# GpSimd's splits and factors in two layers go to VectorE, and its share of the scan's decay masks to ScalarE

## The chip, the core and the metric

The kernel runs on one core of a Trainium2 chip. The engines of the core that matter here are TensorE (PE in the profile, with its weight loads as PEld), VectorE (DVE), ScalarE (ACT) and GpSimd (POOL); SyncE (SP) issues the loads. Each engine works through its own instructions in order, and they wait for one another by semaphores. The metric is the device time of one execution in microseconds (us). Before the change it was 2820.69 us, the median of three runs (2819.77 to 2827.25).

## The reference, cut to what matters

The whole program is two blocks one after the other on 256 tokens of width 1024: a first block of two layers (feed-forward, token mixer, feed-forward), and a second block of two layers, one "even" and one "odd", each a mixer followed by a feed-forward network with a convolution. The change touches the two mixers of the second block.

The even mixer has gated linear attention. Per head it computes, in chunks,

```
cum = jnp.cumsum(lac, axis=1)
rel = jnp.where(tri, cum[:, :, None] - cum[:, None, :], -jnp.inf)
att = jnp.einsum('bthk,bshk,btshk->bhts', qc, kc, jnp.exp(rel))
o = jnp.einsum('bhts,bshv->bthv', att, vc) + jnp.einsum('bthk,bhkv->bthv', qc * jnp.exp(cum), s)
```

in both directions, for the context tokens first and then for the latent tokens, beside an mLSTM scan. The odd mixer has a state-space scan in four groups of eight heads:

```
cum = jnp.cumsum(dtc * A, axis=1)
seg = jnp.where(tri, cum[:, :, None] - cum[:, None, :], -jnp.inf)
cb = jnp.einsum('btgn,bsgn->btsg', cc, bc)
w = jnp.exp(seg) * cb[..., None] * dtc[:, None]
y = jnp.einsum('btsgh,bsghp->btghp', w, xc) + ...
```

Both mixers begin and end with dense products of the tokens with weight matrices in float32.

## The kernel before, in words

**Weights.** Every dense product is made in three passes, from a high and a low part of each operand. A weight tile of 1 MB lands in `raw`; `wsplit` (L411) makes from each half of it the high part `wh` on ScalarE and then the low part `wl` = `raw` - `wh`, a subtraction of 128 x 1024 elements, on VectorE or on GpSimd. Which one is decided by a counter: `lo_pool` = 5 sends every fifth low part to GpSimd, 3 every third, 2 every second, 0 none. It is 0 in the first block, 5 in the even mixer (L1875), 2 in the first convolution network (L1888), 3 in the odd mixer (L1890) and 1.15 in the last network (L1894). There are three buffers each of `raw`, `wh` and `wl`.

**Linear attention** (`gla`, L1218). For each of two pairs of heads and each of two directions it makes the exponentials `Z` (tile `gz`) of seven levels, and then the factors of each level by `factors(i)`: one product of `gz` with the keys on 128 partitions and two with the queries on 64 partitions each, into the tile `gqd`, which has room for four levels. Levels 2 and 5 go to GpSimd, the others to VectorE. `pair_scores` multiplies a level's factors on TensorE and copies the results under a mask to `gs` on VectorE (L830), and asks for the factors of level i + 4 when level i is done. Over context and latents these are 8 passes.

**The scan** (`odd_group`, L1726). For each of 4 groups, 2 token tiles and 2 halves of the heads, the decay exponents of four heads are summed on TensorE in the PSUM tile `aux` from four masked products `oR` (128 x 512): for each direction one from the high part of the decays (`dAh`) on GpSimd, and one from the low part (`dAl`) on VectorE. ScalarE takes the exponential into `oE`, VectorE multiplies it by `oD` (the time steps) and by `cbm`, and TensorE multiplies it with `ox`. `oy`, `oz`, `ow`, `st` and `oss` are the tiles of the rest of the scan; `oss` gets its power -0.5 on GpSimd (`rstd`, L520). Beside it runs `odd_in` of the next group, which evacuates a product `mm` as a convolution into `tof`: one step on ScalarE, two on VectorE, a tanh on ScalarE back into `mm`, and one more step on VectorE.

**Order.** The mixers' generators are woven into one another (`weave`), and a scheduler then lays down each engine's instructions in one fixed order when the program is built. Small powers (`hss`, `mss`, `rsd`, `mv`) stay on GpSimd everywhere.

The helpers are `mul`, `sub` and `tt` (all L173), `stt` (L185), `ts` (L189, L191), `act` (L194) and `mm` (L167), so that most rows of the profile bear a helper's line, and the tile's name tells the place.

Of the kernel before, what the change touches and what calls it, by code (L numbers as in the profile page):

```python
# [14 lines left out]
AF = mybir.ActivationFunctionType  # L15
# [104 lines left out]
class _K:  # L120
# [1096 lines left out]
    def gla(self, o, s, gp, Y):  # L1217

        nc = self.nc
        lah, lal, qT, kT, v, sil = (o[k] for k in ("lah", "lal", "qT", "kT", "v", "sil"))  # L1220
        dirs = (("cf", "sf", 0), ("cb", "sb", 1))

        Q = gp.tile([128, 2, 4, 2, 64], F32, tag="gqd", name="gqd", bufs=1)
        nc.gpsimd.memset(Q, 0.0)
        for j in range(2):
            ZF = gp.tile([128, 2, 2, 128], F32, tag="gzf", name="gzf", bufs=1)

            S = gp.tile([128, 2, 2, 128], F32, tag="gs", name="gs", bufs=1)
            X = gp.tile([128, 2, 2, 128], F32, tag="gx", name="gx", bufs=1)
            nc.gpsimd.memset(S, 0.0)  # L1230
            kv = kT[:, j].rearrange("p (t s) -> p t s", t=2)
            qv = qT[:, j].rearrange("p (t s) -> p t s", t=2)
            for qc, kc, d in dirs:
                Z = gp.tile([128, 2, 8, 128], F32, tag="gz", name="gz", bufs=1)
                cs = slice(d * 256 + j * 128, d * 256 + j * 128 + 128)
                for t in range(2):
                    late = t == (1 - d)
                    mm2 = lambda p, c, tt, a, b: (self.mm(p, lah[:, tt, cs], c, a, False),
                                                  self.mm(p, lal[:, tt, cs], c, False, b))
                    p = self.ps([128, 512], "acc")  # L1240
                    mm2(p, self.lev[:, d * 896:d * 896 + 512], t, True, True)
                    self.act(Z[:, t, 0:4].rearrange("p a b -> p (a b)"), p, AF.Exp)
                    p = self.ps([128, 512], "acc")
                    mm2(p[:, :384], self.lev[:, d * 896 + 512:(d + 1) * 896], t, True, True)
                    mm2(p[:, 384:], self.wr(qc if late else kc), t, True, True)
                    self.act(Z[:, t, 4:8].rearrange("p a b -> p (a b)"), p, AF.Exp)
                    p = self.ps([128, 128], "acc")
                    other = (not late) if s else late
                    mm2(p, self.wr(kc if s else qc), t, True, not other)
                    if other:  # L1250
                        mm2(p, self.wr("ones"), 1 - t, False, True)
                    self.act(ZF[:, d, t], p, AF.Exp)
                    yield
                l_, r_ = (kv, qv) if d == 0 else (qv, kv)
                def factors(i):
                    L = LEVELS[i]
                    eng = nc.gpsimd if i % 3 == 2 else None
                    z, k_, q_ = (self.halves(a, L) for a in (Z[:, :, i, :], kv, qv))
                    self.mul(z[d], z[d], k_[d], eng)
                    for e in range(2):  # L1260
                        pr = slice(e * 64, e * 64 + 64)
                        q = Q[pr, :, i % 4, e].rearrange("p t (b c) -> p t b c", c=L // 2)
                        self.mul(q, z[1 - d][pr], q_[1 - d][pr], eng)
                for i in range(4):
                    factors(i)
                self.mul(Z[:, 0, 7], Z[:, 0, 7], l_[:, 0])
                self.mul(Z[:, 1, 7], Z[:, 1, 7], r_[:, 1])
                self.mul(ZF[:, d], ZF[:, d], kv if s else qv)
                yield
                self.pair_scores(Z, Q, S.rearrange("p e t c -> p (e t) c"), d, kv, qv, factors)  # L1270
                yield
                for e in range(2):
                    pr = slice(e * 64, e * 64 + 64)
                    p = self.ps([128, 128], "acc")
                    self.mm(p, Z[pr, d, 7], Z[pr, 1 - d, 7])
                    self.act(X[:, e, d], p)
                yield
                if s:
                    ke = self.tmp([128, 2, 128], "g")
                    p = self.ps([128, 2, 128], "acc")  # L1280
                    for t in range(2):
                        nc.tensor.transpose(p[:, t], ZF[:, d, t], self.ident)
                    nc.vector.tensor_copy(ke, p)
                    p = self.ps([128, 256], "acc")
                    for t in range(2):
                        self.mm(p, ke[:, t], v[:, t, j * 256:(j + 1) * 256], t == 0, t == 1)
                    nc.vector.tensor_copy(self.gla_state[:, d, j], p)
                    yield
            for e in range(2):
                pr = slice(e * 64, e * 64 + 64)  # L1290
                h = 2 * j + e
                hv = slice(h * 128, h * 128 + 128)
                po = self.ps([128, 2, 128], "acc")
                for t in range(2):
                    self.mm(po[:, t], S[:, e, t], v[:, t, hv], True, False)
                    self.mm(po[:, t], X[:, e, 1 - t], v[:, 1 - t, hv], False, bool(s))
                    if not s:
                        for d in range(2):
                            self.mm(po[:, t], ZF[pr, d, t], self.gla_state[pr, d, j, e * 128:(e + 1) * 128], False, d == 1)
                self.head_norm(po, sil[:, :, hv])  # L1300
                yield
        for _ in self.rows_to_T(sil, [self.col("gla_norm_g_2", k) for k in range(4)], Y, "acc"):
            yield
# [420 lines left out]
    def odd_group(self, o, g, K, gp, Y, big):  # L1724

        nc = self.nc  # L1726
        I32 = mybir.dt.int32
        x, z, BT, Br, CT = (o[k] for k in ("x", "z", "B", "Br", "C"))
# [14 lines left out]
        for d in range(2):  # L1743
            t = d
# [10 lines left out]
        for t in range(2):  # L1755
# [11 lines left out]
            for hq in range(2):  # L1767
                h0 = g * 8 + hq * 4
                pe = self.ps([128, 512], "aux")
                for d, (cc, sc) in enumerate((("cf", "sf"), ("cb", "sb"))):  # L1770
                    for i, a in enumerate(K["dAr"]):
                        R = gp.tile([128, 4, 128], F32R, tag="oR", name="oR", bufs=4)
                        self.mul(R, self.c(cc)[:, None, :].to_broadcast([128, 4, 128]),
                                 self.bc8(a[:, t, d * 32 + h0:d * 32 + h0 + 4], 128), None if i else nc.gpsimd)
                        self.mm(pe, self.wr(sc), R.rearrange("p a b -> p (a b)"), d + i == 0, d + i == 2)
                E = gp.tile([128, 4, 128], F32, tag="oE", name="oE", bufs=1)
                self.act(E.rearrange("p a b -> p (a b)"), pe, AF.Exp)
                dm = gp.tile([128, 4, 128], F32, tag="oD", name="oD", bufs=1)
                self.act(dm, self.bc8(dt[:, t, h0:h0 + 4], 128))
                m = self.c("sf").bitcast(I32)  # L1780
                nc.vector.copy_predicated(out=dm, mask=m[:, None, :].to_broadcast([128, 4, 128]),
                                          data=self.bc8(dt[:, t, 32 + h0:36 + h0], 128))
                self.mul(E, E, dm)
                self.mul(E, E, cbm[:, None, :].to_broadcast([128, 4, 128]))
                for a in range(4):
                    c0 = (hq * 4 + a) * 64
                    self.mm(py[:, c0:c0 + 64], E[:, a], x[:, t, c0:c0 + 64])
                yield
# [75 lines left out]
    def second_block(self):  # L1864

        xc = self.dram.tile([128, 2, D], F32, name="xc")
        with self.tc.tile_pool(name="second", bufs=1) as self.sp:
            with self.tc.tile_pool(name="evenT", bufs=1) as self.hp:
                self.hl = self.pair(self.hp, KT, T, "hl")
                self.operand(5, self.hl)  # L1870
                self.sub_block(5, self.hl, False, lambda: self.load_context(self.sp, self.hp))
                self.run(self.filler)
                self.gctx.__exit__(None, None, None)
                self.r = self.cur
                self.lo_pool = 5  # L1875
                ss, css = self.even(xc)
            self.dump("s000", self.r)
            self.dump("s100", xc)
# [7 lines left out]
    def layers(self, xc, ss):  # L1886
        r = self.r
        self.lo_pool = 2  # L1888
        ss = self.conv_ffn(0, ss, xc)
        self.lo_pool = 3  # L1890
        self.dump("s001", r)
        ss = self.odd()
        self.dump("s010", r)
# [49 lines left out]
```

## Time and profile before

| | before |
|---|---|
| median of three runs | 2820.69 us |
| the profiled execution | 2826.35 us, span 2824.6 us |
| PE busy | 2588.0 us (92%) |
| DVE busy | 2185.3 us (77%) |
| ACT busy | 1238.0 us (44%) |
| POOL busy | 435.0 us (15%) |
| even mixer, 1458 to 1815 us | PE 320.6 of 357 us, DVE 260.4, POOL 68.6 |
| first convolution network, 1852 to 2205 us | PE 353.0 of 353 us |
| odd mixer, 2205 to 2545 us | PE 305.6 of 340 us, DVE 270.2, POOL 92.3 |

Busy times are sums over one engine and say nothing of who waits for whom. The waits of an engine in a stretch do, and the rows of the timeline in which one instruction lasts longer than its like.

### The profile page before, as it was taken

To read this page: it belongs to the slowest core of one execution; us is meant where nothing else is said; L and a number is where in the kernel's file an instruction comes from. 1 tells how busy PE (TensorE), PEld (TensorE's weight loads), DVE (VectorE), ACT (ScalarE), POOL (GpSimd) and SP (SyncE) were. 2 spreads that over 40 slices of the span, in tenths; PEclk is the share of its full clock that TensorE was granted. 3 is DMA by queue.
4 is the path that set the end of the run, shared out by engine and by line. 5 is a ranking of instruction groups with operands and counts; after the bars stand their busy time and mean duration, and the time that the engine had idled before them with its cause. 6 is when DMAs were issued, how large, how long until landed. Compare 5 with 4: busy or idle time off the path is not lost. (4 is left out here: it accounts for less than half of the span.)

```text
span 2824.6 us, 42561 instructions
## 1 busy us (share of the span) xinstructions
PE 2588.0 (92%) x16403; PEld 2287.1 (81%) x16403; DVE 2185.3 (77%) x4073; ACT 1238.0 (44%) x1983; POOL 435.0 (15%) x310
## 2 busy tenths in 40 slices
PE   7997999899899999989998998999999999988887
PEld 6886998799799899879987787778888777757776
DVE  6778997987878999897566857778487478886775
ACT  3444444544444454444445463444233544334443
POOL 0000010000000001000011212212122223234564
PEclk9999999999999999999999999999999999999999
DMA  9898777888888886787572141432223322224443
GB/s 317 284 327 280 243 231 265 261 299 294 279 277 274 269 263 200 257 298 234 187 227 81 34 154 42 151 110 90 90 90 97 102 75 75 83 64 145 141 155 108
DMA packets 374360, 526.31 MB, mean 186 GB/s; under 512 B 24721, under 2 KB 279565, under 8 KB 373005
## 3 DMA queue, kind: packets, MB, share of 16 engines
q1 hardware_dynamic: 372389, 522.83, 56.4%
q8 instruction: 129, 2.11, 0.3%
q10 hardware_dynamic: 1768, 0.76, 0.1%
q14 instruction: 74, 0.61, 0.1%
HBM read 512.46 MB, written 11.08 MB: 185 GB/s over the span
## 5 line engine op out<-in xcount | busy, mean ns | idle before, releaser
L194 ACT ACTIVATE wh<-raw 128x1024 fp32r<-128x1024 f32 x665 | 699.6, 1056 | 916.3 <-PE mm L167 392.5
L173 DVE TENSOR_TENSOR wl<-raw,wh 128x1024 fp32r<-128x1024 f32 (+1 forms) x544 | 666.2, 1229 | 275.8 <-ACT wh L194 272.3
L167 PE MATMUL mm<-hTh,wh 128*128 128x256 f32 (+2 forms) x2200 | 677.0, 308 | 29.0 <-DVE gl L173 8.0
L167 PE MATMUL mm<-hTh,wl 128*128 128x256 f32 (+2 forms) x2200 | 667.1, 303 | 11.4 <-DVE wl L173 11.4
L167 PE MATMUL mm<-hTl,wh 128*128 128x256 f32 (+2 forms) x2200 | 666.9, 303 | 1.3 <-DVE hTl L173 1.3
L167 PEld LDWEIGHTS mm<-hTh,wh 128*128 128x128 f32 (+1 forms) x2200 | 423.0, 192 | 53.6 <-DVE gl L173 10.5
L167 PEld LDWEIGHTS mm<-hTh,wl 128*128 128x128 f32 (+1 forms) x2200 | 422.2, 192 | 30.0 <-DVE wl L173 14.3
L167 PEld LDWEIGHTS mm<-hTl,wh 128*128 128x128 f32 (+1 forms) x2200 | 422.6, 192 | 19.0 <-issue 3.2
L173 POOL TENSOR_TENSOR wl<-raw,wh 128x1024 fp32r<-128x1024 f32 x121 | 293.0, 2426 | 620.3 <-ACT wh L194 594.3
L185 DVE SCALAR_TENSOR_TENSOR graw<-graw,cb 128x1024 f32<-128x1024 f32 x224 | 272.7, 1220 | 36.9 <-DMA graw<-in_c_adaT_dram 31.6
L185 DVE SCALAR_TENSOR_TENSOR fo<-mm,colv,fo 128x189 f32<-128x189 f32 (+3 forms) x396 | 170.1, 430 | 37.6 <-ACT fo L194 35.3
L185 DVE SCALAR_TENSOR_TENSOR fo<-aux,colv,fo 128x189 f32<-128x189 f32 (+3 forms) x396 | 170.2, 430 | 9.7 <-ACT fo L194 6.2
L167 PE MATMUL acc<-wl,gh 128*128 128x512 f32 x352 | 139.2, 395 | 1.6 <-DVE wl L173 1.6
L167 PE MATMUL acc<-wh,gh 128*128 128x512 f32 x352 | 139.5, 396 | 0.6 <-DVE r L173 0.5
L167 PE MATMUL acc<-wh,gl 128*128 128x512 f32 x352 | 138.6, 395 | 0.0
L167 PE MATMUL acc<-wh,cg 128*128 128x512 f32 x396 | 136.2, 403 | 1.9 <-ACT wh L194 1.9
L167 PE MATMUL aux<-hTh,wh 128*128 128x512 f32 (+1 forms) x352 | 120.2, 341 | 14.7 <-DVE cg L173 14.7
L167 PE MATMUL mm<-hlh,wh 128*128 128x256 f32 (+1 forms) x456 | 129.6, 285 | 4.0 <-ACT hlh L194 1.9
L167 PE MATMUL mm<-hlh,wl 128*128 128x256 f32 (+1 forms) x456 | 129.4, 284 | 0.0
L167 PE MATMUL mm<-hll,wh 128*128 128x256 f32 (+1 forms) x456 | 129.1, 283 | 0.0
L167 PE MATMUL aux<-hTh,wl 128*128 128x512 f32 (+1 forms) x352 | 118.8, 338 | 0.0
L167 PE MATMUL mm<-wh,hTh 128*128 128x256 f32 x384 | 112.3, 293 | 7.1 <-ACT hTh L194 3.5
(557 smaller groups left out, 5303.5 us busy)
## 6 DMA issues: line engine op xcount, KB each, us to landing
raw<-in_ffn_w_in_dram SPq DMA_DIRECT2D x88, 1024.0 KB
graw<-in_c_adaT_dram SPq DMA_DIRECT2D x128, 512.0 KB
raw<-in_mix_w_in_dram SPq DMA_DIRECT2D x52, 1024.0 KB
graw<-in_c_modT_dram SPq DMA_DIRECT2D x96, 512.0 KB
raw<-in_ffn_w_up_dram SPq DMA_DIRECT2D x44, 1024.0 KB
raw<-in_ffn_w_out_dram SPq DMA_DIRECT2D x40, 1024.0 KB
raw<-in_even_w_in_dram SPq DMA_DIRECT2D x28, 1024.0 KB
raw<-in_ffn_w_down_dram SPq DMA_DIRECT2D x20, 1024.0 KB
```

The costliest lines, as they stand in the source:

```text
L167: self.nc.tensor.matmul(out, lhsT, rhs, start=start, stop=stop)
L173: (eng or self.nc.vector).tensor_tensor(out=out, in0=a, in1=b, op=op)
L185: self.nc.vector.scalar_tensor_tensor(out, a, s, b, op0=op0, op1=op1, **kw)
L194: self.nc.scalar.activation(out, a, f, **kw)
```

## The change: three edits

The factors of levels 2 and 5 go from GpSimd to VectorE with the others. In the scan, the masked product of the high part becomes four ScalarE instructions of 128 x 128, one for each head, each of which scales the mask by a column. `lo_pool` is 0 in both mixers, so that all their low parts are made on VectorE; the two convolution networks keep theirs.

```diff
                 def factors(i):
                     L = LEVELS[i]
-                    eng = nc.gpsimd if i % 3 == 2 else None
                     z, k_, q_ = (self.halves(a, L) for a in (Z[:, :, i, :], kv, qv))
-                    self.mul(z[d], z[d], k_[d], eng)
+                    self.mul(z[d], z[d], k_[d])
                     for e in range(2):
                         pr = slice(e * 64, e * 64 + 64)
                         q = Q[pr, :, i % 4, e].rearrange("p t (b c) -> p t b c", c=L // 2)
-                        self.mul(q, z[1 - d][pr], q_[1 - d][pr], eng)
+                        self.mul(q, z[1 - d][pr], q_[1 - d][pr])
...
                         R = gp.tile([128, 4, 128], F32R, tag="oR", name="oR", bufs=4)
-                        self.mul(R, self.c(cc)[:, None, :].to_broadcast([128, 4, 128]),
-                                 self.bc8(a[:, t, d * 32 + h0:d * 32 + h0 + 4], 128), None if i else nc.gpsimd)
+                        if i:
+                            self.mul(R, self.c(cc)[:, None, :].to_broadcast([128, 4, 128]),
+                                     self.bc8(a[:, t, d * 32 + h0:d * 32 + h0 + 4], 128))
+                        else:
+                            for h in range(4):
+                                c0 = d * 32 + h0 + h
+                                self.act(R[:, h], self.c(cc), AF.Copy, scale=a[:, t, c0:c0 + 1])
...
                 self.r = self.cur
-                self.lo_pool = 5
                 ss, css = self.even(xc)
...
         ss = self.conv_ffn(0, ss, xc)
-        self.lo_pool = 3
+        self.lo_pool = 0
         self.dump("s001", r)
         ss = self.odd()
```

The scheduler lays the instructions in a new order from the start of the even mixer on. Three places show it.

On GpSimd, from the start of the even mixer into the first passes of linear attention, before:

```order
L523 TENSOR_TENSOR mv<-mv,mhalf 128x1 x2
L173 TENSOR_TENSOR wl<-raw,wh 128x1024
L523 TENSOR_TENSOR rsd<-rsd,mhalf 128x2
L173 TENSOR_TENSOR wl<-raw,wh 128x1024 x2
L173 TENSOR_TENSOR gz<-gz,gk 128x2x16x4
L173 TENSOR_TENSOR gqd<-gz,gq 64x2x64 x2
L173 TENSOR_TENSOR gz<-gz,gk 128x2x2x32
L173 TENSOR_TENSOR gqd<-gz,gq 64x2x64 x2
L1325 MEMSET mll 128x8x2
```

and now:

```order
L523 TENSOR_TENSOR mv<-mv,mhalf 128x1 x2
L523 TENSOR_TENSOR rsd<-rsd,mhalf 128x2
L1324 MEMSET mll 128x8x2
L523 TENSOR_TENSOR mss<-mss,mhalf 128x2
L1230 MEMSET gs 128x512
L523 TENSOR_TENSOR hss<-hss,mhalf 128x2 x2
```

Nothing but memsets and small powers stays on GpSimd there.

On VectorE, the factors of the first pass of linear attention (`gz` and `gqd`, with the width of a level's blocks in the shape), before:

```order
L173 TENSOR_TENSOR gqd<-gz,gq 64x2x64 x2
L173 TENSOR_TENSOR gz<-gz,gk 128x2x32x2
L173 TENSOR_TENSOR gqd<-gz,gq 64x2x64 x2
L173 TENSOR_TENSOR gz<-gz,gk 128x2x8x8
L173 TENSOR_TENSOR gqd<-gz,gq 64x2x64 x2
L173 TENSOR_TENSOR gz<-gz,gq 128x128
L173 TENSOR_TENSOR gzf<-gzf,gk 128x256
L173 TENSOR_TENSOR gz<-gz,gk 128x2x4x16
L173 TENSOR_TENSOR gz<-gz,gk 128x2x64
L173 TENSOR_TENSOR wl<-raw,wh 128x1024
L830 COPY_PREDICATED gs<-mask,acc 128x256
```

and now:

```order
L173 TENSOR_TENSOR gz<-gz,gk 128x2x32x2
L173 TENSOR_TENSOR gqd<-gz,gq 64x2x64 x2
L173 TENSOR_TENSOR gz<-gz,gk 128x2x16x4
L173 TENSOR_TENSOR gqd<-gz,gq 64x2x64 x2
L173 TENSOR_TENSOR gz<-gz,gk 128x2x8x8
L173 TENSOR_TENSOR gqd<-gz,gq 64x2x64 x2
L173 TENSOR_TENSOR gz<-gz,gq 128x128
L173 TENSOR_TENSOR gzf<-gzf,gk 128x256
L830 COPY_PREDICATED gs<-mask,acc 128x256
L173 TENSOR_TENSOR gz<-gz,gk 128x2x4x16
L173 TENSOR_TENSOR gqd<-gz,gq 64x2x64 x2
L173 TENSOR_TENSOR gz<-gz,gk 128x2x2x32
```

Level 2 (blocks of 4, 128x2x16x4) now stands between levels 1 and 3, and level 5 (128x2x2x32) among the masked copies.

On ScalarE, the third step of the scan's first group, with the convolution `tof` of the next group, before:

```order
L194 ACTIVATE wh<-raw 128x1024
L194 ACTIVATE tof<-mm,colv 128x512
L194 ACTIVATE oy,oss<-oz 128x512
L194 ACTIVATE oE<-aux 128x512
L194 ACTIVATE mm<-tof 128x512
L194 ACTIVATE oD<-dt_21818 128x512
L194 ACTIVATE ox<-gv 128x4x128
```

and now:

```order
L194 ACTIVATE wh<-raw 128x1024
L194 ACTIVATE tof<-mm,colv 128x512
L194 ACTIVATE oy,oss<-oz 128x512
L194 ACTIVATE oR<-levr,dAh 128x128 x4
L194 ACTIVATE mm<-tof 128x512
L194 ACTIVATE oR<-levr,dAh 128x128 x4
L194 ACTIVATE oE<-aux 128x512
L194 ACTIVATE oR<-levr,dAh 128x128
L194 ACTIVATE ox<-gv 128x4x128
```

The masked products stand before and behind the tanh (`mm<-tof`), and some before the evacuation of `gv` into `ox`.

## Rows read from the trace of the kernel before

**Rows 1.** The page's first line: the profiled span.
```profile
span 2824.6 us, 42561 instructions
```

**Rows 2.** Stretches: length, busy us of PE, PEld, DVE, ACT, POOL; PEclk, DMA, GB/s.
```profile
1458.00:1815.00 357.00, 320.60 (x2167) 283.29 (x2166) 260.38 (x595) 170.21 (x359) 68.59 (x84) 0.96 0.30 95
1852.00:2205.00 353.00, 353.00 (x1525) 286.33 (x1524) 248.35 (x541) 125.56 (x161) 77.07 (x32) 1.00 0.29 93
2205.00:2545.00 340.00, 305.60 (x1563) 238.44 (x1562) 270.20 (x426) 145.00 (x229) 92.30 (x59) 0.96 0.26 80
```

**Rows 3.** Waits of PE, 1458 to 1815 us: total us, times, longest.
```profile
PE acc L167 <- DVE gqd L173: 5.7, 6, 2.1
...
PE acc L167 <- DVE gs L830: 5.5, 5, 1.9
...
PE aux L1387 <- DVE silu L173: 3.2, 2, 2.8
```

**Rows 4.** Waits of PE, 2205 to 2545 us.
```profile
PE aux L942 <- DVE oz L189: 5.9, 4, 3.1
PE acc L167 <- ACT mm L194: 4.3, 4, 2.1
...
PE gv L1711 <- DVE tof L185: 4.2, 5, 1.6
PE acc L167 <- DVE ow L173: 3.5, 4, 1.6
```

**Rows 5.** Groups on DVE, 2205 to 2545 us: count, busy us, mean ns.
```profile
L173 DVE TENSOR_TENSOR oR<-levr,dAl 128x512 fp32r<-128x512 f32 x32 | 27.6, 874 | 13.9 <-PE aux L167 13.8
...
L173 DVE TENSOR_TENSOR oE<-oE,oD 128x512 f32<-128x512 f32 x16 | 16.6, 1039 | 0.7 <-ACT oE L194 0.7
...
L173 DVE TENSOR_TENSOR oy<-oy,ow 128x512 f32<-128x512 f32 x16 | 10.9, 684 | 0.1
...
L173 DVE TENSOR_TENSOR oy<-ox,coef 128x512 f32<-128x512 f32 x8 | 10.1, 1267 | 0.0
...
L173 DVE TENSOR_TENSOR hTl<-ogy,hTh 128x1024 fp32r<-128x1024 f32 x3 | 3.7, 1218 | 0.3 <-ACT hTh L194 0.3
```

**Rows 6.** Timeline at 2523 us: start, length, instruction, wait before.
```profile
2523.59 2.34 POOL L173 TENSOR_TENSOR wl<-raw,wh 128x1024 fp32r<-128x1024 f32 x1
2523.66 2.56 DVE L189 TENSOR_SCALAR oz<-oz,oss 128x512 f32<-128x512 f32 x1 [0.44 <-POOL oss L523]
...
2526.36 0.45 PE L942 MATMUL aux<-small,oz 128*128 128x128 f32 x1 [3.06 <-DVE oz L189]
```

**Rows 7.** Timeline at 1692 us.
```profile
1691.98 2.36 POOL L173 TENSOR_TENSOR wl<-raw,wh 128x1024 fp32r<-128x1024 f32 x1 [17.28 <-ACT wh L194]
1692.13 2.75 DVE L1368 TENSOR_TENSOR_SCAN g<-small,nmst,g 4x256 f32<-4x256 f32 x1
```

**Rows 8.** Stretches behind PE's longer waits, columns as in rows 2.
```profile
1694.50:1701.00 6.50, 5.55 (x27) 4.75 (x28) 5.84 (x16) 0.57 (x2) 2.86 (x4) 0.50 0.00 0
...
sum 45.00, PE 41.00 PEld 35.98 DVE 32.35 ACT 9.47 POOL 10.66; mean PE 5.12 PEld 4.50 DVE 4.04 ACT 1.18 POOL 1.33
```

**Rows 9.** Groups on POOL, whole span.
```profile
L173 POOL TENSOR_TENSOR wl<-raw,wh 128x1024 fp32r<-128x1024 f32 x121 | 293.0, 2426 | 620.3 <-ACT wh L194 594.3 <-issue 16.4 <-DVE fo L185 9.0
L173 POOL TENSOR_TENSOR oR<-levr,dAh 128x512 fp32r<-128x512 f32 x32 | 41.3, 1305 | 98.8 <-PE aux L167 91.2 <-ACT dAh L194 7.6
```

**Rows 10.** Groups on DVE, 1480 to 1815 us.
```profile
L173 DVE TENSOR_TENSOR gqd<-gz,gq 64x128 f32<-64x128 f32 x80 | 26.0, 325 | 1.0
L173 DVE TENSOR_TENSOR gz<-gz,gk 128x128 f32<-128x128 f32 x48 | 14.8, 314 | 1.9 <-ACT gz L194 1.1
```

**Rows 11.** Groups on ACT of 128 x 128 elements, whole span.
```profile
L194 ACT ACTIVATE krw<-krw,mecols 128x128 f32<-128x128 f32 x16 | 5.9, 397 | 5.5 <-DVE krw L1405 3.0 <-PE aux L167 2.4
...
L194 ACT ACTIVATE dAh<-dA 128x128 fp32r<-128x128 f32 x1 | 0.3, 289 | 0.0
```

**Rows 12.** Waits of ACT, 2205 to 2545 us.
```profile
ACT wh L194 <- PE mm L167: 57.5, 28, 6.5
```

## The prediction

> **What bounds the kernel now.** I read the stretches first. In the first convolution network TensorE is busy for all of its 353 us at the full clock; nothing that another engine does there can shorten it [rows 2]. The two mixers are different: in the even one TensorE stands for 357 - 320.6 = 36.4 us, in the odd one for 340 - 305.6 = 34.4 us, with a granted clock of 0.96 over both [rows 2]. These two stretches are all that the change touches, so 70.8 us of standing, and what the clock loses behind it, is what can be won. VectorE is the engine next to it: 260.4 of 357 and 270.2 of 340 us, 73% and 79%; ScalarE has 48% and 43%, GpSimd 19% and 27% [rows 2].
>
> Next come TensorE's waits in the two stretches. Nearly all are for VectorE or for a ScalarE step that itself stands in a chain with VectorE: in the odd mixer for `oz`, the tanh back into `mm`, `tof` and `ow`, together 5.9 + 4.3 + 4.2 + 3.5 = 17.9 us [rows 4]; in the even one for `gqd`, `gs` and `silu`, 5.7 + 5.5 + 3.2 = 14.4 us [rows 3]. So VectorE's latency sets the pace of the mixers, and not its mean load.
>
> Then the groups of VectorE, to see why it is late. Products of the same form, 128 x 512 from two tiles, take 684 ns in one group (`oy<-oy,ow`), but 874 ns (`oR`), 1039 ns (`oE<-oE,oD`) and 1267 ns (`oy<-ox,coef`) in others [rows 5]. The timeline shows what makes the difference: at 2523.66 us a VectorE step on `oz` lasts 2.56 us, to 2526.22; a low part on GpSimd ran from 2523.59 to 2525.93, and the step ended 0.29 us behind it. TensorE stood 3.06 us for that `oz` [rows 6]. At 1692.13 a prefix sum over four partitions lasts 2.75 us and ends 0.54 us behind a low part on GpSimd [rows 7]; it leads to the wait of 2.8 us for `silu` [rows 3]. VectorE is held up by GpSimd until that one's instruction is over. And the stand has an echo: the stretch behind this wait, and seven like it, run at 0.50 of the clock, the lower of its two levels (1.2 GHz), 45 us in all [rows 8].
>
> **The odd mixer, part by part.** Removed from GpSimd: 32 products `oR` of 1305 ns and, by the order of the new program, 20 of the 31 low parts of 2426 ns that leave it [rows 9]. GpSimd's own time there was no bound. What VectorE gets back: 32 x (874 - 684) = 6.1 us, 16 x (1039 - 684) = 5.7, 8 x (1267 - 684) = 4.7, so 16.5 us from three groups alone [rows 5]. The upper end is GpSimd's busy time there, 92.3 us [rows 2]. I take 30, nearer to the lower end, since other groups have smaller excesses of the same kind. What VectorE gets: 20 low parts at 1218 ns, the price of the same subtraction in `hTl<-ogy,hTh` [rows 5], 24.4 us. So its load stays or falls a little, and pieces of 1.2 us that stand in the order take the place of hold-ups of up to 2 us that no order foresees. What ScalarE gets: 32 x 4 = 128 small products. The old trace has none. The nearest rows are `krw`, 128 x 128 scaled by a column, 397 ns, and `dAh`, a plain copy into the same type, 289 ns [rows 11]: 37 to 51 us. I take 397 ns, since it has the scaling too: 50.8 us, and ScalarE goes from 145 to 196 of 340 us. That is covered as long as ScalarE has the new pieces done while VectorE works on `tof` between the evacuation and the tanh, where the new order puts four of them.
>
> On TensorE: of the 17.9 us above and the smaller waits of the same chains I take 12 as hold-ups that go, since the one in rows 6 alone is worth 2, and 6 us as coming back, as VectorE's known work grows by 24.4 us and ScalarE's queue gets longer. Net -6. Below: nothing goes and 6 come, +6. Above: all of 17.9 go, -17.9.
>
> **The even mixer, part by part.** 11 low parts go to VectorE, 11 x 1.218 = 13.4 us. The factors: 8 passes of two levels each, one product of 314 ns and two of 325 ns [rows 10], 8 x 2 x 0.964 = 15.4 us. That is 28.8 us on VectorE, 260.4 to 289.2 less the hold-ups. Of these the step of rows 7 shows some 2 us; GpSimd's busy time of 68.6 us is the upper end [rows 2]; an estimate from the odd mixer's share, 30 of 92.3, gives 22. So VectorE gets some 7 us more here. On TensorE I take 7 us as going (the waits for `silu` and parts of those for `gqd`), and 5 as coming, since levels 2 and 5 were made beside VectorE and now stand in its line, with the masked copies `gs` and the products that TensorE waits for queued behind them. Net -2; bounds +12 (nothing goes, 12 of the 28.8 us show) and -14.4 (all of the three rows).
>
> **The clock.** The eight stretches of 45 us at 0.50 cost up to half of that, 22.5 us [rows 8], as TensorE was busy for 41 of them. All eight stand in the mixers, behind waits. With the longest waits gone I take a third of it, -8; bounds 0 and -22.5.
>
> **The sum.** -6 - 2 - 8 = -16 us. The profiled execution took 2826.35 us with a span of 2824.6 [rows 1], so it becomes 2810.35. It lies 5.66 us above the median of the runs, 2820.69, so that the median becomes 2804.7, which I round to 2805.
>
> **A rule that speaks against it.** The low parts on GpSimd take 2426 ns on the mean of 121, twice the 1218 ns on VectorE [rows 5, 9], and it is VectorE that was late in both timelines [rows 6, 7]. The Trainium skill, in "SBUF — State Buffer", section "Who interferes with whom", says that a VectorE instruction with two SBUF inputs contends with a GpSimd one that reads SBUF, and that whoever issues first keeps the port while the other blocks. By that rule GpSimd could be the one that waits as often as VectorE; then half of my 30 and 22 us of hold-ups would not be VectorE's, the added 53.2 us would outweigh the rest, and the result would be the second case below. The trace agrees with the blocking; the excess of three groups in rows 5, which already is 16.5 us, says that VectorE loses often.
>
> **The rivals.**
>
> *The added load eats the gain.* VectorE gets 24.4 + 28.8 = 53.2 us of work and gets back some 30 + 22 = 52. If a hold-up in TensorE's shadow is exchanged for a subtraction in its path as often as the reverse, the time stays 2821. For it: the two sums are equal. Against it: the added pieces are in the order that the scheduler plans with, and the hold-ups stand right before TensorE's longest waits.
>
> *ScalarE becomes late in the scan.* ScalarE stands 57.5 us in 28 waits for TensorE to free a buffer of high parts [rows 12]; a product `oR` queued behind one is late, and the exponents in `aux` with it. If each of the 16 steps loses two of its instructions, 16 x 2 x 0.397 = 12.7 us, 3 us are left of the gain: 2817.
>
> *Linear attention gets slower.* VectorE is in series with TensorE in each of the 8 passes: exponentials, factors, products, masked copies. If nothing covers the 28.8 us there, and only the 7 us of hold-ups go, the even mixer gets 22 us longer; with nothing won elsewhere 2843. It decides if TensorE's waits for `gqd` and `gs`, 11.2 us now [rows 3], rise by more than the 16 us that I expect to win. For it: VectorE's 73%, on one chain. Against it: dense products from the other woven generators stand between.
>
> *Everything is given back.* The 12 and 7 us go, nothing comes, and the clock never falls: -41.5 us, 2779.
>
> **How the numbers follow.** My forecast gets 0.52, the load that eats the gain 0.20, ScalarE 0.09, linear attention 0.12, everything given back 0.07. Less than 0.3%, 8.5 us, can't be told from no change here. The forecast's own spread, 2792 to 2815, lies below 2812.2 but for a small part, so faster is 0.49 + 0.07 and a little of the ScalarE case, 0.58; within it is 0.29; slower is linear attention and a little, 0.13. The range is 2786 to 2829: below it most of the last case, above it most of the linear attention case.
>
> **What would show it.** Right: `oE<-oE,oD` and `oy<-ox,coef` at about 684 ns, no prefix sum of 2.75 us, TensorE's waits for `oz` under 3 us in all, fewer stretches at half clock in the mixers, and the first network's 353 us as before. Wrong: longer waits for `gqd` or `gs`; waits of TensorE for `oR` from ScalarE; the three groups still slow, which would mean that GpSimd was not the cause.

## The result and the profile after

The changed kernel takes 2776.43 us, the median of four runs (2769.46 to 2786.78), against 2820.62 us before in the same comparison: a ratio of 0.9844 (95% interval 0.9825 to 0.9863), 44 us faster. Forecast were 16 us and a range down to 2786; the time lies 10 us below the range. The profiled execution was the slowest of the four, 2786.78 us with a span of 2785.0.

To see where the time went, both spans are cut at the same instructions: a power `mv` at the end of the first block, a power `rsd` before the first network and one on either side of the odd mixer, and the end. The columns are those of [rows 2]. Before, the four stretches are the even mixer with what follows it up to the first network, that network, the odd mixer, and the last network:

```profile
1461.00:1838.00 377.00, 335.78 (x2222) 294.66 (x2221) 273.00 (x610) 181.74 (x378) 72.90 (x87) 0.96 0.33 106
1838.00:2221.00 383.00, 375.75 (x1621) 304.27 (x1621) 268.63 (x577) 141.14 (x191) 80.79 (x35) 0.99 0.29 94
2221.00:2575.00 354.00, 318.95 (x1619) 248.98 (x1617) 274.92 (x426) 149.98 (x231) 101.12 (x62) 0.97 0.28 86
2575.00:2824.00 249.00, 206.23 (x1336) 186.09 (x1336) 170.17 (x434) 110.51 (x170) 130.81 (x57) 0.92 0.40 134
```

and after:

```profile
1468.00:1835.00 367.00, 336.71 (x2224) 294.42 (x2223) 278.01 (x670) 182.69 (x378) 19.10 (x28) 0.97 0.34 109
1835.00:2217.00 382.00, 374.51 (x1618) 303.30 (x1617) 268.39 (x575) 141.21 (x191) 78.07 (x34) 0.99 0.29 95
2217.00:2545.00 328.00, 311.93 (x1619) 245.32 (x1617) 264.62 (x445) 186.27 (x359) 10.74 (x11) 0.98 0.29 92
2545.00:2784.00 239.00, 204.36 (x1336) 185.78 (x1336) 168.28 (x433) 110.18 (x170) 134.61 (x58) 0.92 0.41 139
```

The even stretch is 10 us shorter, the first network the same to 1 us, the odd mixer 26 us shorter and the last network, up to the end of the span, 9.6 us shorter, though no line of it changed: 46 us in all. The first block, also unchanged, took 7 us more in this execution (the even mixer starts at 1468 in place of 1461 us), so that the two spans differ by 39.6 us.

In the odd mixer TensorE stood for 354 - 319.0 = 35 us before and for 328 - 311.9 = 16 us after; its work, the same 1619 instructions, took 7.0 us less, at a granted clock of 0.98 in place of 0.97. In the two mixers there are now five longer stretches at the lower clock, 28.6 us, where [rows 8] had eight and 45 us (columns as there):

```profile
1512.70:1515.60 2.90, 2.90 (x15) 2.90 (x15) 2.90 (x5) 2.59 (x3) 0.00 (x0) 0.50 0.20 66
...
sum 28.60, PE 28.43 PEld 25.61 DVE 19.96 ACT 10.09 POOL 0.86; mean PE 5.69 PEld 5.12 DVE 3.99 ACT 2.02 POOL 0.17
```

VectorE has 19 instructions more in its count and is busy for 10.3 us less. As 19 low parts of 1.22 us were added to it, 23.2 us, some 33 us of its busy time went. Its groups show where; the second to fourth answer to the three slow ones of [rows 5]:

```profile
L173 DVE TENSOR_TENSOR wl<-raw,wh 128x1024 fp32r<-128x1024 f32 x54 | 65.9, 1221 | 34.5 <-ACT wh L194 34.5
...
L173 DVE TENSOR_TENSOR oR<-levr,dAl 128x512 fp32r<-128x512 f32 x32 | 21.9, 684 | 0.8 <-PE aux L167 0.8
...
L173 DVE TENSOR_TENSOR oE<-oE,oD 128x512 f32<-128x512 f32 x16 | 11.0, 687 | 3.1 <-ACT oE L194 3.1
...
L173 DVE TENSOR_TENSOR oy<-ox,coef 128x512 f32<-128x512 f32 x8 | 5.5, 685 | 0.0
```

874, 1039 and 1267 ns have become 684, 687 and 685. The products that went to ScalarE:

```profile
L194 ACT ACTIVATE oR<-levr,dAh 128x128 fp32r<-128x128 f32 x128 | 42.4, 392 | 0.0
```

392 ns each (397 were taken, [rows 11]), but only 42.4 us busy, as neighbours overlap. TensorE's waits in the odd mixer, total, times and longest, beside [rows 4]:

```profile
PE gv L1710 <- DVE tof L185: 3.5, 4, 1.8
PE aux L167 <- DVE oR L173: 2.4, 2, 2.0
...
PE aux L942 <- DVE oz L189: 0.5, 2, 0.3
```

The waits for `oz` went from 5.9 to 0.5 us, that for the tanh in `mm` (4.3) is gone. In the even mixer, beside [rows 3]:

```profile
PE gv L167 <- DVE mE L173: 4.4, 5, 1.2
...
PE aux L1386 <- DVE silu L173: 1.8, 4, 0.9
...
PE acc L167 <- DVE gs L830: 1.1, 4, 0.4
PE acc L167 <- DVE gqd L173: 0.8, 3, 0.3
```

The waits for `gqd`, `gs` and `silu`, 14.4 us before, are 3.7 us; `mE`, of the mLSTM, is now the longest in total. The prefix sum that had lasted 2.75 us [rows 7] takes 0.73 us:

```profile
1693.96 1.21 DVE L173 TENSOR_TENSOR wl<-raw,wh 128x1024 fp32r<-128x1024 f32 x1
1695.10 0.73 DVE L1367 TENSOR_TENSOR_SCAN g<-small,nmst,g 4x256 f32<-4x256 f32 x1
```

A low part now stands before it on VectorE and takes 1.21 us, where the hold-up, 2.75 against 0.73, was 2.0.

### The profile page after: what moved, and what is told of

It is laid out like the page before. It is cut to its first block, busy times and chain, and to the rows that moved or that the text cites. A ratio compares the mean times of both kernels' runs of the same rounds, so it can differ in the third digit from the quotient of the medians.

```text
span 2785.0 us, 42594 instructions
## 1 busy us (share of the span) xinstructions
PE 2580.8 (93%) x16403; PEld 2284.0 (82%) x16403; DVE 2177.8 (78%) x4152; ACT 1275.3 (46%) x2111; POOL 292.9 (11%) x199
## 5 line engine op out<-in xcount | busy, mean ns | idle before, releaser
L173 DVE TENSOR_TENSOR wl<-raw,wh 128x1024 fp32r<-128x1024 f32 (+1 forms) x575 | 700.4, 1222 | 259.6 <-ACT wh L194 257.1
L173 POOL TENSOR_TENSOR wl<-raw,wh 128x1024 fp32r<-128x1024 f32 x90 | 216.9, 2415 | 415.3 <-ACT wh L194 406.5
L167 PE MATMUL aux<-hTl,wh 128*128 128x512 f32 (+1 forms) x352 | 120.5, 342 | 0.0
```

The costliest lines, as they stand in the source:

```text
L167: self.nc.tensor.matmul(out, lhsT, rhs, start=start, stop=stop)
L173: (eng or self.nc.vector).tensor_tensor(out=out, in0=a, in1=b, op=op)
```

## The experiments

The theory is that VectorE was late because GpSimd's instructions held it up, and that this time lay in TensorE's path. Rivals: the new order pays, or VectorE's load matters and the gain comes from elsewhere. "Before" is always the kernel before, run in the same comparison (medians 2824.8, 2828.2 and 2825.7 us in the three), and a ratio is against it, with its 95% interval. A stretch is read from one profiled execution. Stretches whose code did not change between kernels show how far that goes: the odd mixer with the lines of before takes 353 to 358 us in five profiles, and with those of the change 326 to 328 in three. So 4 us in a stretch are hardly more than its spread.

**The parts one by one.** First the odd mixer's low parts alone.

```diff
-        self.lo_pool = 3
+        self.lo_pool = 0
...
-        self.lo_pool = 1.15
+        self.lo_pool, self.nsplit = 1.15, 0.4
```

> The kernel before with one part of the change alone: lo_pool 0 in the odd mixer, so that its 19 low parts on GpSimd go to VectorE. The counter is set to 0.4 at the start of the last network, where it stands in the kernel before, so that network stays as it was. Theory (hold-ups): VectorE loses time only while GpSimd reads SBUF, and the odd mixer's gain of 26 us is that time; the low parts hold VectorE up for about half of it, so the run is 10 to 15 us faster than before and the scan's groups (oy<-ox,coef above all) get shorter, while those that overlap the scan's masked products on GpSimd stay long. Rival (order): the new order of instructions pays, not the missing hold-ups; then one part alone gives any sign, within 5 us of before. Rival (load): 23 us more on VectorE in the mixer, 0 to 10 us slower.

Measured: 0.9938 (0.9915 to 0.9961), 17 us faster, a little more than the theory's 10 to 15. The odd mixer:

```profile
2218.00:2560.00 342.00, 316.91 (x1616) 246.78 (x1614) 277.53 (x442) 149.18 (x231) 56.82 (x45) 0.97 0.29 88
```

12 us shorter, though VectorE is busier than before, 277.5 against 274.9 us. As 23.2 us of low parts came to it, 20.6 us of hold-ups went. The run gives only the sum of the two: what went was worth 12 us more than what came cost.

Then the masked products alone, as in the diff of the change.

> The kernel before with only the scan's masked products of the high part moved from GpSimd to ScalarE. Theory (hold-ups): the 32 products on GpSimd held VectorE up for about 15 us, 10 to 15 us faster than before; VectorE's oR at 684 ns where no low part overlaps it. Rival (ScalarE late): 128 small pieces in ScalarE's line delay the evacuations, 0 to 10 us slower and TensorE waits for oR from ScalarE.

Measured: 0.9927 (0.9906 to 0.9949), 20 us faster, more than the theory's 10 to 15; the odd mixer takes 335 us, 19 less:

```profile
2220.00:2555.00 335.00, 312.18 (x1618) 246.25 (x1616) 254.54 (x425) 185.26 (x359) 57.54 (x31) 0.97 0.29 91
```

VectorE is busy for 20.4 us less, and 19 come out of the stretch: TensorE stands for 22.8 us in place of 35.1, and its own work takes 6.8 us less. ScalarE, 35 us busier, is not late; TensorE waits 2.0 us for its `oR`:

```profile
PE aux L167 <- ACT oR L194: 2.0, 2, 1.5
```

The even mixer's two parts together:

```diff
-                self.lo_pool = 5
...
-                    eng = nc.gpsimd if i % 3 == 2 else None
...
-        self.lo_pool = 2
+        self.lo_pool, self.nsplit = 2, 0.4
```

> The kernel before with the even mixer's parts alone: factors and low parts of the even mixer on VectorE (the counter set to 0.4 behind it, so that later stages stay as they were). Theory (hold-ups): the even mixer's 9 us between the two profiles are all due to it, 7 to 12 us faster. Rival (load): VectorE's 29 us more show in linear attention, 0 to 10 us slower, and the 9 us came from elsewhere.

Measured: 0.9955 (0.9937 to 0.9973), and the stretch 13 us shorter:

```profile
1462.00:1826.00 364.00, 333.89 (x2225) 290.72 (x2224) 277.39 (x671) 182.84 (x378) 19.02 (x28) 0.98 0.35 110
```

Of these, the factors alone (the lines of `factors` in the change and nothing else):

> The kernel before with only the factors of levels 2 and 5 moved from GpSimd to VectorE. GpSimd's factors held VectorE up by about 9 us and cost VectorE 14 us when it makes them. Theory (hold-ups): the even mixer, 377 us with what follows up to the first network, becomes 2 to 6 us shorter; the rest of its 11 to 13 us comes from the low parts. Rival (load): 0 to 8 us longer, as the factors stand in the chain that TensorE waits for.

Measured: 1.0022 (1.0009 to 1.0034), slower if anything, with the stretch at 378 us:

```profile
1462.00:1840.00 378.00, 337.62 (x2218) 293.54 (x2217) 278.49 (x657) 181.75 (x378) 47.47 (x39) 0.96 0.33 106
```

The theory's 2 to 6 us did not come, and the rival's range holds the result. Its reason is not borne out: TensorE's waits for `gqd` and `gs`, 11.2 us before, are 5.2 here, and those for `msig`, of the mLSTM, went from 3.8 to 6.7:

```profile
PE aux L942 <- DVE msig L173: 6.7, 5, 3.0
...
PE acc L167 <- DVE gs L830: 2.8, 6, 1.2
...
PE acc L167 <- DVE gqd L173: 2.4, 4, 1.2
```

And the low parts alone (`lo_pool` 5 taken out, the counter at 0.4 behind it):

> The kernel before with only the low parts of the even mixer moved from GpSimd to VectorE (the counter set to 0.4 behind it). They held VectorE up by about 11 us, in single steps of up to 2 us. Theory (hold-ups): 5 to 10 us shorter, and the waits of TensorE behind the long prefix sum go. Rival (load): within 3 us of before, since VectorE gets 15 us more.

Measured: 0.9965 (0.9952 to 0.9977), 367 us:

```profile
1457.00:1824.00 367.00, 333.47 (x2221) 293.54 (x2220) 274.19 (x622) 181.84 (x378) 47.14 (x75) 0.97 0.34 109
```

So most of the even mixer's gain is that of its 12 low parts; the long prefix sum goes with them, too. Whether the factors add to it beside them (0.9955 against 0.9965) is not shown: the even stretch is 367 us here and 361 to 367 in the eight profiles with both parts.

**The last network.** The counter of low parts carries its rest from one part of the program to the next.

```diff
-        self.lo_pool = 1.15
+        self.lo_pool, self.nsplit = 1.15, 0.0
```

> The kernel before with the counter of the low parts set to 0.0 at the start of the last network, where it stands at 0.4 before and at 0.0 in the changed kernel; nothing else. In the profiles the last network takes 249 us before and 240 after, though no line of it changed. Theory (phase): which of its low parts go to GpSimd depends on that rest, and this alone is worth 7 to 10 us. Rival (spread): the 9 us are a difference of two executions, and the time stays within 3 us of before.

Measured: 0.9973 (0.9960 to 0.9986), 8 us faster, and the network at 239 us with nothing else changed:

```profile
2576.00:2815.00 239.00, 203.59 (x1336) 184.54 (x1336) 168.14 (x433) 110.35 (x170) 134.70 (x58) 0.93 0.42 139
```

TensorE's waits in it, before:

```profile
PE aux L167 <- DVE cg L173: 14.7, 11, 3.3
PE acc L167 <- DVE wl L173: 6.9, 2, 4.0
```

and with the rest at 0:

```profile
PE aux L167 <- DVE cg L173: 9.6, 9, 1.9
PE aux L167 <- DVE wl L173: 4.6, 1, 4.6
```

The reverse, the changed kernel with the rest put back to 0.4:

> The changed kernel with the counter of the low parts set to 0.4 at the start of the last network, where it stands in the kernel before. Theory (phase): the last network goes back from 240 to 249 us and the time is 7 to 10 us above the changed kernel; the rest of the gain, about 35 us, is the mixers'. Rival: the network's gain came from how the odd mixer ends, and the time stays within 3 us of the changed kernel.

Measured: 2787.42 us, 0.9852 (0.9832 to 0.9871). In the profile the network is back at 247 us and the odd mixer stays at 328:

```profile
2209.00:2537.00 328.00, 311.40 (x1618) 244.58 (x1616) 263.25 (x442) 186.18 (x359) 13.56 (x13) 0.98 0.30 92
2537.00:2784.00 247.00, 205.61 (x1336) 185.25 (x1336) 170.18 (x433) 110.50 (x170) 130.35 (x57) 0.92 0.41 135
```

The ratio, 0.9852 against 0.9844, does not show the 8 us; the stretches do. Over all runs the last network takes 247 to 250 us in the seven profiles with the rest at 0.4, and 239 or 240 in the seven with 0. The ratio shows something else: with the rest held the change still gains some 41 us, so the two mixers carry most of it.

**GpSimd's work put back without its use.** The results of GpSimd's instructions here go to a tile `idle` that nobody reads. The first line runs for every third split (the counter is left out), the second for each of the 32 masked products of the high part.

```diff
+            self.sub(j, r, hl[0].bitcast(F32), self.nc.gpsimd)
...
+                            self.mul(j, R.bitcast(F32), self.bc8(a[:, t, d * 32 + h0:d * 32 + h0 + 4], 128), nc.gpsimd)
```

> The changed kernel, and in the odd mixer GpSimd does useless work beside it, of the size that it had before: every third split it subtracts again into a tile that nobody reads (128 x 1024), and for each of the 32 masked products of the high part it multiplies 128 x 512 into the same tile. Nothing waits for the results; the buffers that it reads come free a little later. Theory (hold-ups): VectorE is held up again by 20 to 30 us as before, and the odd mixer takes 12 to 26 us longer than in the changed kernel (328 us). Rival (order): GpSimd's work costs only where something waits for its result; then the time stays within 5 us of the changed kernel.

Measured: 2809.14 us, 0.9937 (0.9916 to 0.9957). The odd mixer takes 360 us, 32 more than in the changed kernel and more than the theory's 12 to 26, and VectorE is busy for 302.8 us in place of 264.6:

```profile
2209.00:2569.00 360.00, 321.60 (x1617) 247.28 (x1615) 302.83 (x443) 186.72 (x359) 104.31 (x62) 0.97 0.28 85
```

The same places, with memsets, each row of them behind a product of 128 x 1 that ties it to the same moment:

```diff
+            self.sub(self.junk[:, 0:1], r[:, 0, 0:1], hl[0][:, 0, 0:1].bitcast(F32), self.nc.gpsimd)
+            for n in (1024, 1024, 512):
+                self.nc.gpsimd.memset(self.junk[:, :n], 0.0)
...
+                            self.mul(self.junk[:, 0:1], R[:, 0, 0:1].bitcast(F32), a[:, t, 0:1], nc.gpsimd)
+                            for n in (1024, 320):
+                                nc.gpsimd.memset(self.junk[:, :n], 0.0)
```

> As the run with useless work on GpSimd in the odd mixer, but the work is memsets for about the same time (three for a split, two for a masked product), each behind one product of 128 x 1 elements that ties it to the same moment. Theory (hold-ups): what holds VectorE up is GpSimd's reading of SBUF, so that writes alone cost nothing: VectorE's groups as short as in the changed kernel, and the odd mixer within 4 us of its 328. Rival (any work of GpSimd holds VectorE up): as with the reads, 12 to 26 us longer.

Measured: 2784.34 us, 0.9855 (0.9832 to 0.9877). GpSimd is busier than with the reads, 121.9 us (88.7 of them memsets, where the useless reads took 94.1), and the odd mixer takes 332 us:

```profile
2205.00:2537.00 332.00, 310.67 (x1616) 242.85 (x1615) 265.41 (x443) 186.22 (x359) 121.92 (x184) 0.99 0.30 93
```

One group of VectorE in the two runs, with the reads:

```profile
L174 DVE TENSOR_TENSOR oE<-oE,oD 128x512 f32<-128x512 f32 x16 | 16.3, 1020 | 1.5 <-ACT oE L195 1.5
```

and with the writes:

```profile
L174 DVE TENSOR_TENSOR oE<-oE,oD 128x512 f32<-128x512 f32 x16 | 11.0, 686 | 1.5 <-ACT oE L195 1.5
```

That settles it against the rival of the order. VectorE goes through the odd mixer as in the changed kernel, with 441 of its 444 instructions in the same order beside the reads and 435 beside the writes, and the work that nobody waits for costs 32 us if it reads SBUF and 4 us if it nearly only writes. The reads also hold their buffers longer: loads of `raw` stand for 29.8 us behind `idle`, 18.6 with the writes. TensorE does not wait for that. Its waits, with the reads, are for VectorE's tiles, and 0.4 us for a low part:

```profile
PE aux L168 <- DVE oR L174: 9.8, 7, 4.2
PE gv L1716 <- DVE tof L186: 6.3, 7, 1.8
PE aux L948 <- DVE oz L190: 3.2, 4, 2.2
...
PE acc L168 <- DVE wl L174: 0.4, 1, 0.4
```

The Trainium skill, "SBUF — State Buffer", section "Who interferes with whom", says that VectorE with two SBUF inputs contends with a GpSimd instruction that reads SBUF, and not with one that only writes; the two runs agree, 1020 against 686 ns in this group.

**What VectorE's own work costs.** The masked products on VectorE in place of ScalarE:

```diff
-                        if i:
...
-                                self.act(R[:, h], self.c(cc), AF.Copy, scale=a[:, t, c0:c0 + 1])
+                        self.mul(R, self.c(cc)[:, None, :].to_broadcast([128, 4, 128]),
+                                 self.bc8(a[:, t, d * 32 + h0:d * 32 + h0 + 4], 128))
```

> The changed kernel, with the scan's masked products of the high part on VectorE too, as one instruction of 684 ns each instead of four on ScalarE: 32 x 0.684 = 21.9 us more on VectorE in the odd mixer, 42 us less on ScalarE, nothing more on GpSimd. Theory (hold-ups): VectorE's work that stands in the planned order is cheaper than the same time of hold-ups; the odd mixer gets 3 to 12 us longer than in the changed kernel and stays well below the 354 us before. Rival (load): VectorE is in series with TensorE, and the 22 us show almost whole, 18 us or more.

Measured: 2791.45 us, 0.9868 (0.9846 to 0.9890), with the odd mixer at 346 us:

```profile
2207.00:2553.00 346.00, 318.61 (x1619) 249.79 (x1617) 284.29 (x477) 150.18 (x231) 11.24 (x12) 0.96 0.28 88
```

18 us more for 19.7 us of VectorE: the rival's number, not the theory's 3 to 12. Then the same amount as subtractions of splits:

```diff
+            self.sub(j, r, hl[0].bitcast(F32))
```

> The changed kernel, and in the odd mixer VectorE subtracts every third split a second time into a tile that nobody reads: 19 x 1.22 = 23 us more on VectorE, nothing on GpSimd. VectorE then gets as much as by the low parts that the change gave it, once more. Theory (low parts hide): subtractions of the splits are made ahead of TensorE, in gaps of VectorE, and cost the odd mixer 0 to 8 us of its 328, unlike the scan's masked products, of which 22 us on VectorE cost 18. Rival (all of VectorE's time counts): 15 us or more.

Measured: 2780.26 us, 0.9851 (0.9833 to 0.9870), with the odd mixer at 332 us:

```profile
2205.00:2537.00 332.00, 315.78 (x1620) 248.82 (x1618) 284.17 (x464) 186.25 (x359) 12.18 (x12) 0.97 0.30 93
```

VectorE is as busy as in the run before, 284.2 against 284.3 us, and TensorE finishes 14 us sooner. So the sum of VectorE's work does not decide. That the kind of work does is argued and not shown: nobody reads these subtractions, while TensorE waits for the masked products, and in both runs the scheduler also laid the odd mixer in another order than in the changed kernel.

**A further step.** The first block has factors on GpSimd too.

```diff
-                self.zmul(Z, i, L, kv, qv, eng=nc.gpsimd if i % 3 == 2 else None)
+                self.zmul(Z, i, L, kv, qv)
```

> The changed kernel with the same edit in the first block: the 32 factors of its scan (hz) that GpSimd makes, 732 to 749 ns each, go to VectorE at about 278 ns. They hold VectorE up by some 4 us in all there. Theory: 0 to 4 us faster than the changed kernel, too little to tell in one comparison. Rival (load): VectorE gets 9 us more where TensorE is never without work, no change either; slower by 5 or more would mean that it stands in TensorE's path.

Measured: 2771.27 us, 0.9818 (0.9800 to 0.9836). It is faster than the kernel before; against the changed kernel (0.9844) the intervals overlap, so it is not shown to be better.

## Why the prediction was wrong

**What bounds the kernel** was right. Most of the gain is in TensorE's standing in the mixers, GpSimd's instructions were the cause, and the signs named are there: the three groups near 684 ns, no prefix sum of 2.75 us, `oz` under 3 us, fewer stretches at half clock, the first network unchanged.

**The odd mixer, net -6, is the first step that failed.** Of the waits, 12 us were to go and 6 to come; TensorE's standing fell by 19 us (35.1 to 16.1), more than the 17.9 of the upper bound. The size of the hold-ups was right, 30 us taken and 33 gone. Their price in standing was too low, 12 of 30 us, taken from the waits that [rows 4] names. With the masked products alone 20.4 us less on VectorE took 12.2 us of standing away, and with the useless reads 38.2 us more brought 22.3 (16.1 to 38.4): in both, 0.6 of the hold-up. TensorE's own work moved with it, by 6.8 and 9.7 us, so that 19 of 20.4 and 32 of 38.2 us showed in the stretch. The 6 us that were to come, for VectorE's added work and ScalarE's longer queue, were too high: 0.6 of 33 is 20, of which 19 showed, which leaves about 1 as an estimate, and 19.6 us of subtractions more (264.6 to 284.2) left the standing at 16.2 us. Why they cost so little stays open: that low parts are made ahead of need and fill VectorE's gaps fits, but no run isolates it.

**The even mixer, net -2,** came out at -10.9 us of standing (41.2 to 30.3). The 7 us that were to go were too few, and the 5 that were to come are not seen in the sum. The low parts alone took 7.7 us of standing away and gave 10 us of time by 0.9965. The factors alone changed the standing by 0.8 us and gave nothing (1.0022). The prediction had put their price into the waits for `gqd` and `gs`; these fell.

**The clock, -8,** was about right: the counted stretches at half clock went from 45 to 28.6 us, and the same TensorE work took 7.0 us less in the odd mixer and 0.9 us more in the even one.

**The last network was not in the sum at all.** I had limited the change to the two mixers. Taking out `lo_pool` there leaves the rest of the counter at 0 in place of 0.4, which shifts which low parts of the last network go to GpSimd: 8 us by the comparison that changed nothing else. The rest shows in the code, and I had also split the 31 low parts as 11 and 20, where they are 12 and 19. But this term is not what took the time out of the range: with the rest held at 0.4 the ratio is at most 0.9871 by its interval, and that of 2820.6 is 2784 us, still below 2786.

**The rivals.** "Everything is given back", 2779, came nearest by its number and got 0.07, but not by its mechanism: the clock gave 6 to 8 of its 22.5 us, and 8 came from the last network; that it came near is luck. ScalarE did not become late: no wait of TensorE for its `oR` is among those of the changed kernel. The load did not eat the gain. The rule on who issues first did not turn the result: GpSimd loses time too (2720 ns in the useless subtractions against 2415 over the changed kernel's low parts), but VectorE's loss is what TensorE sees:

```profile
L174 POOL TENSOR_TENSOR idle<-raw,wh 128x1024 f32<-128x1024 f32 (+1 forms) x19 | 51.7, 2720 | 124.9 <-ACT wh L195 99.4 <-issue 22.1 <-ACT nc L195 3.0
```

from the run with reads, and from the changed kernel:

```profile
L173 POOL TENSOR_TENSOR wl<-raw,wh 128x1024 fp32r<-128x1024 f32 x90 | 216.9, 2415 | 415.3 <-ACT wh L194 406.5
```

**What stays open.** Why the phase of the counter is worth 8 us in the last network is shown only as fewer waits for `cg` and `wl`, not taken apart; other rests were not tried. Whether the factors should stay on GpSimd in the changed kernel was not tried either.

## What to carry to other kernels

Before an engine's work is moved, look at the same form of instruction in several groups: a mean of 1039 beside 684 ns was here the sign that another engine was in the way. On the engine that TensorE waited for, such time came out of the stretch almost whole, 19 of 20.4 us. Load that is added to that engine can't be priced by its sum: 20 us of it cost 18 us of the stretch in one run and 4 in another. A guess from these runs, not shown, is that work made ahead into buffers hides and work between two products of TensorE does not. A counter or a rotation that runs through the whole program carries an edit into parts that the edit does not name.

## What the runs showed that was not expected

Small instructions are held up like large ones: a prefix sum of 4 x 256 lasted 2.75 us beside a low part of 2.36 us on GpSimd, and 0.73 without one. GpSimd can be busy for 122 of 332 us beside VectorE at almost no cost, if nearly all of it is writing; of VectorE's groups of several instructions `oz<-oz,oss` alone was clearly longer then, 596 ns against 486. And the first block, with the same instructions in all of these kernels but the last, ends between 1457 and 1468 us in the profiled executions, so that a span alone can't tell 10 us.
